# State updates as 32-row tiles and a stacked fp32r attention product in a gated-linear-attention layer

## Chip, cores and metric

One Trainium2 chip, one core. The metric is the device time of one execution in microseconds, the median of several runs. Below, PE is the engine of the matrix products (PEld its weight loader), DVE the vector engine, ACT the scalar engine, POOL the GpSimd engine, SP the engine whose queue issues most weight transfers.

## The reference

One decoder layer runs for a prompt (256 tokens) and for eight sample sequences of eight tokens each, with shared weights. The part that the change touches is the samples' gated linear attention, per head of 256 key and 512 value channels:

```python
b = jnp.cumsum(loga, axis=3)
b_last = b[:, :, :, -1:, :]
qe = q * jnp.exp(b)
ke = k * jnp.exp(-b)
kd = k * jnp.exp(b_last - b)
decay = jnp.exp(b_last[:, :, :, 0, :])
att = jnp.where(mask, jnp.einsum('nbhcd,nbhsd->nbhcs', qe, ke), 0.0)
o_intra = jnp.einsum('nbhcs,nbhse->nbhce', att, v)
def step(s, inp):
    qe_n, kd_n, v_n, dec_n = inp
    o = jnp.einsum('bhcd,bhde->bhce', qe_n, s)
    s = dec_n[..., None] * s + jnp.einsum('bhcd,bhce->bhde', kd_n, v_n)
    return s, o
```

Around it stand the input projection, the pooling branch, the merge by gates, the output projection and a SwiGLU feed-forward part; all of it is computed in float32.

## The kernel before

**The large products.** Tokens lie in the free dimension (256 of the prompt and 64 of the samples, 320 columns), channels in the partitions. Each weight chunk is split by ACT (L152) into a rounded part `whi` and by DVE (L153) into the rest `wlo`; `mm3` (L190 to L192) then makes three fp32r products of 128x128 weights with 320 columns. PE does hardly anything else from start to end. The weights come over SP's queue, in chunks into a ring of buffers.

**The heads.** While the projections of head h run (h = 1 to 3, then the output projection), the attention of the head before is worked off in steps from a queue (`gla_steps`, `pool_steps`). `pump` writes the steps between the projections, but a scheduler of the framework decides in which order each engine gets the instructions; it moves single products in between those of `mm3`. Conditioning vectors are made alongside by `ada_step` (L242, products of 128x32 column tiles on `w_ada`).

**The samples.** The eight sequences are two groups (gg) of four; each sequence has a slot of 32 partitions. `s_vstack` fills a slot with four copies of its eight value rows, in the order rounded part, rest, rounded part, rest; after the transposes of `s_nat2` that is `vp`. `s_prod` makes `kdP`, the keys that feed the state: 16 rows of rounded parts, 16 rows of rests. So one product over a slot's 32 rows gives the four cross terms.

- `s_nat3` transposes `kdP` and copies it (L886) into `kpz`: for each of the four slots j a whole 128-row array, zero outside the slot's 32 rows. Two copies on DVE and two on ACT, of 32 partitions each; the zeros are written once, on POOL (L719).
- `s_state` makes, for each group, each half d of the key channels and each sequence, one fp32r product of 128 rows and 512 columns (L957), into a PSUM tile of its own from a ring of four (`misc`), and updates the state on DVE (L959): 64 products in all, two per step.
- `s_attP` makes the scores of four sequences at once (L916) and copies them under a mask (L919) into `attP`; its rows beyond the first 16 of a slot are zero.
- `s_inter` multiplies `attP` by `vp` in float32 (L932), which PE runs as two passes, and adds the products of `qeP` with the loaded states as column tiles of 128x32, four next to each other (L936). `s_oback` copies the result out (L943) and transposes it back (L129, tile `osn`).

Other products that use less than the full array: `s_gk` (L745 and L746, 48 rows: the gate's rank and its bias) and `s_att` (L843, column tiles).

```python
PE.matmul(pt, lhsT=kpz[:, gg, j, d * P:(d + 1) * P], rhs=E["vp"][:, gg], start=True, stop=True)
...
PE.matmul(pt, lhsT=attP[:, gg], rhs=E["vp"][:, gg].bitcast(F32), start=True, stop=False,
```

Of the kernel before, what the change touches and what calls it, by code (L numbers as in the profile page):

```python
# [11 lines left out]
F32 = mybir.dt.float32  # L12
F32R = mybir.dt.float32r
I32 = mybir.dt.int32
AF = mybir.ActivationFunctionType
ALU = mybir.AluOpType
# [4 lines left out]
P = 128  # L21
TP, NB, LS = 256, 8, 8
# [6 lines left out]
H, DK, DV = 4, 256, 512  # L29
# [13 lines left out]
def shape_constants():  # L43
    s = np.arange(P)[:, None]
    c = np.arange(P)[None, :]
    m = 32 * (c // 32) + 15
    dq = ((s > m) & (s <= c)).astype(np.float32) - ((s > c) & (s <= m)).astype(np.float32)
    e = np.zeros((P, 4, 4), np.float32)
    for j in range(4):
        for i in range(j + 1, 4):  # L50
            sv = np.arange(P)
            e[:, j, i] = (sv > 32 * j + 15) & (sv <= 32 * i + 15)
    e = e.reshape(P, 16)
    after = (s > c).astype(np.float32)
    upto = (s <= c).astype(np.float32)
    m0 = np.concatenate([dq, after, e], 1)
    m1 = np.concatenate([dq, after, upto, e], 1)
    ss = np.arange(TS)[:, None]
    cs = np.arange(TS)[None, :]
    same = (ss // LS) == (cs // LS)  # L60
    ms = np.zeros((P, 2 * TS), np.float32)
    ms[:TS, :TS] = same & (ss <= cs)
    ms[:TS, TS:] = same & (ss > cs)
    inv = np.zeros((P, 4, 16), np.float32)
    for g, w in enumerate(WINDOWS):
        inv[:, g] = (1.0 / np.minimum(np.arange(16) + 1, w).astype(np.float32))[None]
    cf = np.concatenate([inv.reshape(P, 64), m0, m1, ms], 1).astype(np.float32)
    mask = (s <= c).astype(np.int32)
    r = np.arange(P)[:, None]
    q = np.arange(P)[None, :]  # L70
    mp = ((r // 32 == q // 32) & ((r % 32) < 16) & ((q % 32) < 8)
          & ((r % 8) <= (q % 32))).astype(np.int32)
    ci = np.concatenate([mask, mp], 1).astype(np.int32)
    return np.ascontiguousarray(cf), np.ascontiguousarray(ci)


NM0, NM1, NMS = 272, 400, 128
CFW = NM0 + NM1 + NMS + 64


def body(tc, A):
    nc = tc.nc
    ctx = ExitStack()
    cp = ctx.enter_context(tc.tile_pool(name="cp", bufs=1))
# [12 lines left out]
    def nm(s):  # L97
        uid[0] += 1
        return "%s_%d" % (s, uid[0])

    def misc():
        return pmisc.tile([P, 512], F32, tag="m", name=nm("pm"))
# [1 line left out]
    V, S, G, PE = nc.vector, nc.scalar, nc.gpsimd, nc.tensor  # L104


    cst = cp.tile([P, 2 * P + 64], F32, name="cst")
    msk = cp.tile([P, 2 * P], I32, name="msk")
    ident = cst[:, 0:P]
    ones = cst[:, P:2 * P]  # L110
    V.memset(ones, 1.0)
    invc = cst[:, 2 * P:2 * P + 64]
    cumr = cp.tile([P, NM0 + NM1 + NMS], F32R, name="cumr")
    M0, M1, MS = cumr[:, 0:NM0], cumr[:, NM0:NM0 + NM1], cumr[:TS, NM0 + NM1:NM0 + NM1 + NMS]
    epst = cp.tile([P, 1], F32, name="epst")
# [6 lines left out]
    vec = cp.tile([P, 4 * KT + 4], F32, name="vec")  # L122
    N1G, N2G, FG, PSC, GNG = vec[:, 0:16], vec[:, 16:32], vec[:, 32:48], vec[:, 48:64], vec[:, 64:68]
    alr = cp.tile([48, T], F32, name="alr")
    cp.tile([P, 40], F32, name="lpad")

    def tr(out, in_):
        k = in_.shape[0]
# [274 lines left out]
    with tc.tile_pool(name="head", bufs=1) as xp:  # L403
# [34 lines left out]
        pt = misc()  # L438
# [8 lines left out]
        def pinned(ins):  # L447
            tc.keep_in_program_order(ins)
# [77 lines left out]
        pt = misc()  # L526
# [118 lines left out]
        def late_loads():  # L645
            pinned(nc.gpsimd.dma_start(walr, win[:, :, OAL:OAL + 16]))
            pinned(nc.gpsimd.dma_start(msk, A["ci"]))
            pinned(nc.gpsimd.dma_start(cum, A["cf"][:, 64:CFW]))
            pinned(nc.gpsimd.dma_start(invc, A["cf"][:, 0:64]))


        plan = {}
# [60 lines left out]
    lp = mix.enter_context(tc.tile_pool(name="lp", bufs=1))  # L713
    qeP = lp.tile([P, 2, NB, 32], F32, name="qeP")
    keP = lp.tile([P, 2, NB, 32], F32, name="keP")
    kpz = lp.tile([P, 2, 4, DK], F32R, name="kpz")
    attT = lp.tile([P, 3, P], F32, name="attT")
    attP = lp.tile([P, 2, P], F32, name="attP")
    G.memset(kpz.bitcast(F32), 0.0)  # L719
    G.memset(qeP, 0.0)  # L720
    G.memset(keP, 0.0)
    G.memset(attT, 0.0)
    G.memset(attP, 0.0)

    def w4(shape, dt=F32):
        return lp.tile(shape, dt, tag="w4", bufs=4, name=nm("w4"))
# [1 line left out]
    def gla_steps(g):  # L728
        h = g.h
        st = []  # L730
        E = {}
# [57 lines left out]
        def s_prod():  # L789
            EQ, EK, EX, q, k = E["EQ"], E["EK"], E["EX"], g.q, g.k  # L790
            for d in range(2):
                V.tensor_tensor(qeP[:, d, :, 0:LS], s3(EQ[:, d, TP:T]), s3(q[:, d, TP:T]), op=ALU.mult)
                kk = s3(k[:, d, TP:T])
                V.tensor_tensor(keP[:, d, :, 0:LS], s3(EK[:, d, TP:T]), kk, op=ALU.mult)
                V.tensor_copy(E["dec"][:, d], s3(EQ[:, d, TP:T])[:, :, LS - 1])
            for d in range(2):
                G.tensor_copy(keP[:, d, :, LS:2 * LS], keP[:, d, :, 0:LS])
            V.tensor_tensor(EX[:, :, 416:480], EX[:, :, 416:480], k[:, :, TP:T], op=ALU.mult)
            kdP = E["kdP"] = w4([P, 2, NB, 32], F32R)
            for d in range(2):  # L800
                kd4 = kdP[:, d].rearrange("p b (c t) -> p b c t", t=LS)
                kd = s3(EX[:, d, 416:480]).unsqueeze(2).broadcast_to([P, NB, 2, LS])
                V.tensor_copy(kd4[:, :, 0:2, :], kd)
                V.tensor_tensor(kd4[:, :, 2:4, :], kd, kd4[:, :, 0:2, :].bitcast(F32), op=ALU.subtract)
            V.tensor_tensor(EQ[:, :, 0:TP], EQ[:, :, 0:TP], q[:, :, 0:TP], op=ALU.mult)
            V.tensor_tensor(EK[:, :, 0:TP], EK[:, :, 0:TP], k[:, :, 0:TP], op=ALU.mult)
            kq = w4([P, 2, 2, P])
            E["kdA"], E["q2"] = kq[:, 0], kq[:, 1]
            V.tensor_tensor(EX[:, :, 0:P], EX[:, :, 0:P], k[:, :, 0:P], op=ALU.mult)
            V.tensor_tensor(EX[:, :, 144:272], EX[:, :, 144:272], k[:, :, P:TP], op=ALU.mult)  # L810
            V.tensor_tensor(E["q2"], EX[:, :, 272:400], q[:, :, P:TP], op=ALU.mult)
            for d in range(2):
                V.tensor_scalar(E["kdA"][:, d], EX[:, d, 0:P], EX[:, d, 399:400], None, op0=ALU.mult)
# [58 lines left out]
        def s_nat3():  # L872
            pt = misc()
            for d in range(2):
                tr(pt[:, d * P:(d + 1) * P], E["kdA"][:, d])
                tr(pt[:, DK + d * P:DK + (d + 1) * P], E["EX"][:, d, 144:272])
            kdn = w4([P, 2, DK])
            V.tensor_copy(kdn, pt.rearrange("p (s d) -> p s d", s=2))
            pt = misc()
            for gg in range(2):  # L880
                for d in range(2):
                    tr(pt[:, gg * DK + d * P:gg * DK + (d + 1) * P],
                       E["kdP"][:, d, 4 * gg:4 * gg + 4, :].rearrange("p b r -> p (b r)").bitcast(F32))
            for j in range(4):
                r = slice(32 * j, 32 * j + 32)
                (S.copy if j % 2 else V.tensor_copy)(kpz[r, :, j, :], pt[r].rearrange("p (s d) -> p s d", s=2))  # L886
            E["kdn"] = kdn

        def s_o(e2):
# [22 lines left out]
        def s_attP():  # L912
            for gg in range(2):
                pt = misc()
                for d in range(2):
                    PE.matmul(pt[:, 0:P], lhsT=keP[:, d, 4 * gg:4 * gg + 4, :].rearrange("p b r -> p (b r)"),  # L916
                              rhs=qeP[:, d, 4 * gg:4 * gg + 4, :].rearrange("p b r -> p (b r)"),
                              start=d == 0, stop=d == 1)
                V.copy_predicated(attP[:, gg], msk[:, P:2 * P], pt[:, 0:P])  # L919

        def s_load(gg, d):
            def f():
# [6 lines left out]
        def s_inter(gg):  # L929
            def f():  # L930
                pt = E["oi"] = misc()
                PE.matmul(pt, lhsT=attP[:, gg], rhs=E["vp"][:, gg].bitcast(F32), start=True, stop=False,  # L932
                          skip_group_check=True)
                for d in range(2):
                    for j in range(4):
                        PE.matmul(pt[32 * j:32 * j + 32, :], lhsT=qeP[:, d, 4 * gg + j, :], rhs=E["S0", gg, d][:, j],  # L936
                                  start=False, stop=d == 1, tile_position=(0, 32 * j), skip_group_check=True)
            return f
# [13 lines left out]
        def s_state(gg, d, j0):  # L952
            def f():
                t = E["S0", gg, d]
                for j in (j0, j0 + 1):
                    pt = misc()
                    PE.matmul(pt, lhsT=kpz[:, gg, j, d * P:(d + 1) * P], rhs=E["vp"][:, gg], start=True, stop=True)  # L957
                    c = 4 * gg + j
                    V.scalar_tensor_tensor(t[:, j], t[:, j], E["dec"][:, d, c:c + 1], pt, op0=ALU.mult, op1=ALU.add)  # L959
                if j0 == 2:  # L960
                    nc.gpsimd.dma_start(A["o_gs"][0, 4 * gg:4 * gg + 4, h, d * P:(d + 1) * P, :]
                                        .rearrange("b p e -> p b e"), t)
            return f
# [393 lines left out]
```

## Time and profile before

| what | value |
|---|---|
| median of 3 runs | 1979.95 us (1979.15 to 1981.06) |
| the profiled execution's own time | 1981.86 us |
| its span (first to last instruction) | 1980.1 us |
| PE busy | 1946.9 us, 15080 instructions |
| PEld busy | 1857.3 us |
| DVE busy | 1014.6 us |
| ACT busy | 819.0 us |
| POOL busy | 136.5 us |

A busy time counts from an instruction's start to its modelled end. PE's products overlap, so their durations are longer than the distance between their starts; where PE's time goes is read from the starts in the timeline, and from the idle time ahead of an instruction with what ended it.

### The profile page before, as it was taken

To read this page: it belongs to the slowest core of one execution; us is meant where nothing else is said; L and a number is where in the kernel's file an instruction comes from. 1 tells how busy PE (TensorE), PEld (TensorE's weight loads), DVE (VectorE), ACT (ScalarE), POOL (GpSimd) and SP (SyncE) were. 2 spreads that over 40 slices of the span, in tenths; PEclk is the share of its full clock that TensorE was granted. 3 is DMA by queue.
4 is the path that set the end of the run, shared out by engine and by line. 5 is a ranking of instruction groups with operands and counts; after the bars stand their busy time and mean duration, and the time that the engine had idled before them with its cause. 6 is when DMAs were issued, how large, how long until landed. Compare 5 with 4: busy or idle time off the path is not lost.

```text
span 1980.1 us, 37312 instructions
## 1 busy us (share of the span) xinstructions
PE 1946.9 (98%) x15080; PEld 1857.3 (94%) x15080; DVE 1014.6 (51%) x1896; ACT 819.0 (41%) x1468; POOL 136.5 (7%) x257
## 2 busy tenths in 40 slices
PE   8999999999999999999999999999999999999997
PEld 6889998898999899889999999999999999999997
DVE  3566675575446534664574444444444444444554
ACT  3333374364345433643354333333333434344443
POOL 1112220111010101010030000000000000000000
PEclk9999999999999999999999999999999999999998
DMA  9987555776975787579656665444444444444443
GB/s 312 364 292 262 170 172 154 264 250 203 318 239 180 285 273 222 173 252 322 224 169 213 202 214 192 149 149 144 158 144 152 150 150 150 151 151 144 150 141 94
DMA packets 324607, 400.84 MB, mean 202 GB/s; under 512 B 13545, under 2 KB 264681, under 8 KB 324097
## 3 DMA queue, kind: packets, MB, share of 16 engines
q1 hardware_dynamic: 312002, 357.68, 56.2%
q0 software_dynamic: 12432, 40.77, 5.6%
q8 instruction: 118, 1.93, 0.4%
q14 instruction: 55, 0.45, 0.1%
HBM read 373.96 MB, written 24.67 MB: 201 GB/s over the span
## 4 chain that ended last, share of the span: by engine, by line
PE 94%; DMA 3%; DVE 1%; ACT 1%; issue 0%; POOL 0%; SPq 0%; POOLq 0%; DVEq 0%; ACTq 0%
PE ps L190 27%; PE ps L191 27%; PE ps L192 27%; PE pm L242 5%; DMA raw<-w_ada 1%; PE pm L129 1%; DMA raw<-w_o 1%; PE pm L936 1%; PE pm L957 1%; PE pm L905 1%; DMA raw<-w_in 1%; PE pm L435 1%; PE idle L431 1%; PE pm L932 0%; PE pm L894 0%
## 5 line engine op out<-in xcount | busy, mean ns | idle before, releaser
L153 DVE TENSOR_TENSOR wlo<-raw,whi 128x512 fp32r<-128x512 f32 x948 | 656.1, 696 | 790.7 <-ACT whi L152 787.4
L152 ACT CAST whi<-raw 128x512 fp32r<-128x512 f32 x948 | 584.4, 621 | 980.7 <-PE ps L191 865.9
L190 PE MATMUL ps<-hh,whi 128*128 128x320 f32 x1408 | 442.4, 314 | 6.6 <-ACT whi L152 5.2
L192 PE MATMUL ps<-hh,wlo 128*128 128x320 f32 x1408 | 439.2, 312 | 0.0
L191 PE MATMUL ps<-hl,whi 128*128 128x320 f32 x1408 | 438.6, 312 | 0.0
L190 PE MATMUL ps<-h2h,whi 128*128 128x320 f32 x1408 | 435.8, 310 | 0.0
L191 PE MATMUL ps<-h2l,whi 128*128 128x320 f32 x1408 | 434.9, 309 | 0.8 <-DVE h2l L1227 0.8
L192 PE MATMUL ps<-h2h,wlo 128*128 128x320 f32 x1408 | 434.8, 309 | 0.0
L190 PEld LDWEIGHTS ps<-hh,whi 128*128 128x128 f32 x1408 | 265.3, 188 | 21.6 <-issue 10.4
L191 PEld LDWEIGHTS ps<-hl,whi 128*128 128x128 f32 x1408 | 265.4, 189 | 7.2 <-issue 5.9
L192 PEld LDWEIGHTS ps<-hh,wlo 128*128 128x128 f32 x1408 | 265.2, 188 | 6.8 <-issue 5.5
L190 PEld LDWEIGHTS ps<-h2h,whi 128*128 128x128 f32 x1408 | 264.1, 188 | 2.4 <-issue 2.2
L191 PEld LDWEIGHTS ps<-h2l,whi 128*128 128x128 f32 x1408 | 264.3, 188 | 1.1 <-DVE h2l L1227 1.1
L192 PEld LDWEIGHTS ps<-h2h,wlo 128*128 128x128 f32 x1408 | 264.3, 188 | 0.0
L190 PE MATMUL ps<-ah,whi 128*128 128x320 f32 x704 | 218.5, 310 | 0.0
L192 PE MATMUL ps<-ah,wlo 128*128 128x320 f32 x704 | 217.7, 309 | 0.0
L191 PE MATMUL ps<-al,whi 128*128 128x320 f32 x704 | 217.6, 309 | 0.0
L191 PEld LDWEIGHTS ps<-al,whi 128*128 128x128 f32 x704 | 132.2, 188 | 0.0
L190 PEld LDWEIGHTS ps<-ah,whi 128*128 128x128 f32 x704 | 132.2, 188 | 0.0
L192 PEld LDWEIGHTS ps<-ah,wlo 128*128 128x128 f32 x704 | 132.2, 188 | 0.0
L242 PE MATMUL pm<-raw,scT 128*32 128x128 f32 (+1 forms) x2688 | 101.5, 293 | 4.3 <-DMA raw<-w_ada 4.3
L242 PEld LDWEIGHTS pm<-raw,scT 128*32 128x32 f32 x2688 | 72.0, 110 | 25.7 <-issue 13.4
(315 smaller groups left out, 1569.3 us busy)
## 6 DMA issues: line engine op xcount, KB each, us to landing
raw<-w_ada SPq DMA_DIRECT2D x192, 512.0 KB, 6.3
raw<-w_gu SPq DMA_DIRECT2D x176, 512.0 KB, 3.5
raw<-w_in SPq DMA_DIRECT2D x173, 512.0 KB, 4.3
raw<-w_down SPq DMA_DIRECT2D x79, 512.0 KB, 3.4
S<-state_gla POOLq DMA_DIRECT2D x16, 1024.0 KB, 8.9
o_gs<-S POOLq DMA_DIRECT2D x16, 1024.0 KB, 7.3
raw<-w_o SPq DMA_DIRECT2D x32, 512.0 KB, 5.6
raw<-w_down SPq DMA_DIRECT2D x15, 256.0 KB, 2.5
```

What stands on the lines that cost most here:

```text
L129: PE.transpose(out, in_, ident[:k, :k])
L152: S.copy(hi, raw)
L153: V.tensor_sub(lo, raw, hi.bitcast(F32))
L190: PE.matmul(ps, lhsT=whi, rhs=xhi, start=start, stop=False)
L191: PE.matmul(ps, lhsT=whi, rhs=xlo, start=False, stop=False)
L192: PE.matmul(ps, lhsT=wlo, rhs=xhi, start=False, stop=stop)
L242: ins = PE.matmul(ps[32 * j:32 * j + 32, 0:w], lhsT=scT[:, k, :], rhs=raws[j], start=k == 0 if start is None else start, stop=k == KT - 1 ...
L431: tc.keep_in_program_order(PE.matmul(idle[:, 0, :], lhsT=fill[:, 0:P], rhs=fill, start=True, stop=True))
L435: tc.keep_in_program_order(PE.transpose(out, in_, ident[:k, :k]))
L905: PE.matmul(pt, lhsT=E["kdn"][:, s, d * P:(d + 1) * P], rhs=E["vn"][:, s], start=s == 0, stop=s == 1)
L936: PE.matmul(pt[32 * j:32 * j + 32, :], lhsT=qeP[:, d, 4 * gg + j, :], rhs=E["S0", gg, d][:, j], start=False, stop=d == 1, tile_position=(0 ...
L957: PE.matmul(pt, lhsT=kpz[:, gg, j, d * P:(d + 1) * P], rhs=E["vp"][:, gg], start=True, stop=True)
```

## The change

1. `kpz` and its zeros go. One ACT copy (L887 after) puts the transposed keys into `kp`, 128 partitions with the four slots below each other.
2. `s_state` takes two PSUM tiles and issues its two products on the slots' 32 partitions alone, as row tiles (`tile_position=(32 * j, 0)`), and then the two updates.
3. The keys of the scores (`keP`) are repeated over all four parts of a slot instead of two, by POOL, and the mask keeps all 32 rows. `ahl` holds the masked scores. ACT rounds them into `attP` (L921), ACT makes `ah`, the rounded part with a sign by row (L923), and DVE combines (L924), so that the first 16 rows of a slot hold the rounded scores and the last 16 the rest. With `vp` as it was, one fp32r product then gives the four cross terms (L937).

```diff
-    kpz = lp.tile([P, 2, 4, DK], F32R, name="kpz")
+    kp = lp.tile([P, 2, DK], F32R, name="kp")
+    ahl = lp.tile([P, 2, P], F32, name="ahl")
...
-                G.tensor_copy(keP[:, d, :, LS:2 * LS], keP[:, d, :, 0:LS])
+                G.tensor_copy(keP[:, d].rearrange("p b (c t) -> p b c t", t=LS)[:, :, 1:4, :],
+                              keP[:, d, :, 0:LS].unsqueeze(2).broadcast_to([P, NB, 3, LS]))
...
-            for j in range(4):
-                r = slice(32 * j, 32 * j + 32)
-                (S.copy if j % 2 else V.tensor_copy)(kpz[r, :, j, :], pt[r].rearrange("p (s d) -> p s d", s=2))
+            S.copy(kp, pt.rearrange("p (s d) -> p s d", s=2))
...
-                V.copy_predicated(attP[:, gg], msk[:, P:2 * P], pt[:, 0:P])
+                V.copy_predicated(ahl[:, gg], msk[:, P:2 * P], pt[:, 0:P])
+                S.copy(attP[:, gg], ahl[:, gg])
+                t = lp.tile([P, P], F32, tag="acc", name=nm("ah"))
+                S.activation(t, attP[:, gg].bitcast(F32), AF.Copy, scale=adds)
+                V.scalar_tensor_tensor(attP[:, gg], ahl[:, gg], takes, t, op0=ALU.mult, op1=ALU.add)
...
-                PE.matmul(pt, lhsT=attP[:, gg], rhs=E["vp"][:, gg].bitcast(F32), start=True, stop=False,
+                PE.matmul(pt, lhsT=attP[:, gg], rhs=E["vp"][:, gg], start=True, stop=False,
...
-                for j in (j0, j0 + 1):
-                    pt = misc()
-                    PE.matmul(pt, lhsT=kpz[:, gg, j, d * P:(d + 1) * P], rhs=E["vp"][:, gg], start=True, stop=True)
+                pts = [misc() for _ in range(2)]
+                for j, pt in zip((j0, j0 + 1), pts):
+                    r = slice(32 * j, 32 * j + 32)
+                    PE.matmul(pt, lhsT=kp[r, gg, d * P:(d + 1) * P], rhs=E["vp"][r, gg], start=True, stop=True,
+                              tile_position=(32 * j, 0))
+                for j, pt in zip((j0, j0 + 1), pts):
                     c = 4 * gg + j
                     V.scalar_tensor_tensor(t[:, j], t[:, j], E["dec"][:, d, c:c + 1], pt, op0=ALU.mult, op1=ALU.add)
```

The rest of the diff makes the mask and the two columns of row signs (`takes`, `adds`), loads them, and drops the zero fill.

**The order of the instructions.** PE in the first head, second half of the key channels, before (L957 is a state product, L190 to L192 are projections, `ps` is their result):

```order
L190 MATMUL ps_3934<-hh_93,whi_3953 128x320
L191 MATMUL ps_3934<-hl_803,whi_3953 128x320
L957 MATMUL pm_3862<-vp_3578,kpz 128x512
L192 MATMUL ps_3934<-hh_93,wlo_3954 128x320
L190 MATMUL ps_3934<-hh_94,whi_3971 128x320
L191 MATMUL ps_3934<-hl_1184,whi_3971 128x320
L957 MATMUL pm_3865<-vp_3578,kpz 128x512
L192 MATMUL ps_3934<-hh_94,wlo_3972 128x320
```

and after (L963 is the state product, L192 to L194 the projections):

```order
L192 MATMUL ps_3939<-hh_93,whi_3958 128x320
L193 MATMUL ps_3939<-hl_803,whi_3958 128x320
L963 MATMUL pm_3865<-vp_3578,kp 128x512
L194 MATMUL ps_3939<-hh_93,wlo_3959 128x320
L192 MATMUL ps_3939<-hh_94,whi_3976 128x320
L193 MATMUL ps_3939<-hl_1184,whi_3976 128x320
L963 MATMUL pm_3870<-vp_3578,kp 128x512
L194 MATMUL ps_3939<-hh_94,wlo_3977 128x320
```

Nothing moved here: the products still stand one by one between projections, now as row tiles.

PE in the second head, behind the transposes of `s_oback`, before:

```order
L190 MATMUL ps_5218<-hh_96,whi_5271 128x320
L129 MATMUL pm_4713<-cst,osn_4711 128x128 x4
L957 MATMUL pm_4722<-vp_4664,kpz 128x512
L957 MATMUL pm_4725<-vp_4664,kpz 128x512
L957 MATMUL pm_4728<-vp_4664,kpz 128x512
L191 MATMUL ps_5218<-hl_1245,whi_5271 128x320
```

and after (L131 are the transposes):

```order
L192 MATMUL ps_5228<-hh_97,whi_5281 128x320
L131 MATMUL pm_4723<-cst,osn_4721 128x128 x4
L963 MATMUL pm_4732<-vp_4669,kp 128x512
L963 MATMUL pm_4733<-vp_4669,kp 128x512
L963 MATMUL pm_4738<-vp_4669,kp 128x512
L193 MATMUL ps_5228<-hl_1269,whi_5281 128x320
```

The run of three state products stays a run of three, two projections later.

ACT in the first head, where the scores' new steps come in, after (L154 are the weight casts):

```order
L154 CAST whi_3792<-raw_3790 128x512
L887 CAST kp<-pm_3598 128x512
L921 CAST attP<-ahl 128x128 x2
L923 ACTIVATE ah_3609<-attP,cst 128x128
L154 CAST whi_3808<-raw_3790 128x512
L923 ACTIVATE ah_3617<-attP,cst 128x128
L154 CAST whi_3942<-raw_3940 128x512
```

Before, two copies to `kpz` stood among these casts, and nothing for the scores.

## Rows read from the trace of the kernel before

**Rows 1.** The page: busy time by engine, and the chain that ended last.
```profile
PE 1946.9 (98%) x15080; PEld 1857.3 (94%) x15080; DVE 1014.6 (51%) x1896; ACT 819.0 (41%) x1468; POOL 136.5 (7%) x257
...
PE 94%; DMA 3%; DVE 1%; ACT 1%; issue 0%; POOL 0%; SPq 0%; POOLq 0%; DVEq 0%; ACTq 0%
```

**Rows 2.** PE's groups by form: busy us, mean ns | idle before.
```profile
L957 PE MATMUL pm<-vp,kpz 128*128 128x512 f32 x64 | 23.2, 405 | 0.0
...
L932 PE MATMUL pm<-vp,attP 128*128 128x512 f32 x16 | 8.3, 598 | 0.0
```

**Rows 3.** Timeline of PE around a state product: start us, us, instruction.
```profile
347.18 0.31 PE L191 MATMUL ps<-hl,whi 128*128 128x320 f32 x1
347.32 0.39 PE L957 MATMUL pm<-vp,kpz 128*128 128x512 f32 x1
347.56 0.31 PE L192 MATMUL ps<-hh,wlo 128*128 128x320 f32 x1
347.70 0.31 PE L190 MATMUL ps<-hh,whi 128*128 128x320 f32 x1
```

**Rows 4.** The tile kpz: ns min/median/max, and idle before (us, times).
```profile
L957 PEld LDWEIGHTS pm<-vp,kpz x64: 186/188/192, 338.7 to 870.8; 128*128 128x128 f32 x64
...
L886 DVE CAST kpz<-pm x8: 671/684/690, 327.3 to 820.5; 32x512 fp32r<-32x512 f32 x8
L886 ACT CAST kpz<-pm x8: 576/577/579, 328.0 to 821.2; 32x512 fp32r<-32x512 f32 x8
...
  issue: 0.2, 1
```

**Rows 5.** Timeline of PE around the gate stage of a head.
```profile
587.32 0.31 PE L190 MATMUL ps<-hh,whi 128*128 128x320 f32 x1
587.56 1.13 PE L745 MATMUL pm<-wa,alr 48*128 48x256 f32 x4
588.62 0.64 PE L746 MATMUL pm<-wa,alr 48*64 48x256 f32 x2
589.19 0.41 PE L191 MATMUL ps<-hl,whi 128*128 128x320 f32 x1
589.44 0.31 PE L192 MATMUL ps<-hh,wlo 128*128 128x320 f32 x1
```

**Rows 6.** Timeline of DVE, PE and PEld around the first head's attention product.
```profile
328.79 0.48 DVE L919 COPY_PREDICATED attP<-msk,pm 128x128 f32<-128x128 int32 x2
...
331.77 0.31 PE L191 MATMUL ps<-hl,whi 128*128 128x320 f32 x1
...
331.92 1.02 PE L932 MATMUL pm<-vp,attP 128*128 128x512 f32 x2
...
332.87 1.92 PE L936 MATMUL pm<-S,qeP 128*32 128x512 f32 x16
...
334.72 0.19 PEld L192 LDWEIGHTS ps<-hh,wlo 128*128 128x128 f32 x1 [0.84 <-issue]
334.72 0.41 PE L192 MATMUL ps<-hh,wlo 128*128 128x320 f32 x1
...
334.97 0.31 PE L190 MATMUL ps<-hh,whi 128*128 128x320 f32 x1
```

**Rows 7.** Waits of the weight loader: us in total, times, longest.
```profile
PEld pm L242 <- issue: 13.4, 66, 0.4
PEld pm L936 <- issue: 7.9, 21, 0.8
...
PEld pm L746 <- issue: 1.3, 4, 0.3
```

**Rows 8.** ACT's groups by form, 235 to 900 us.
```profile
L851 ACT COPY attT<-pm 128x128 f32<-128x128 f32 x4 | 1.1, 265 | 8.9 <-PE pm L848 8.9
```

**Rows 9.** Waits of PE: us in total, times, longest.
```profile
PE pm L242 <- DMA raw<-w_ada: 4.3, 3, 2.3
...
PE ps L190 <- ACT mh L327: 0.9, 1, 0.9
```

More of the change, by code (lines that the diff above doesn't have):

```diff
@@ L66, in shape_constants @@
         inv[:, g] = (1.0 / np.minimum(np.arange(16) + 1, w).astype(np.float32))[None]
-    cf = np.concatenate([inv.reshape(P, 64), m0, m1, ms], 1).astype(np.float32)
+    lo = s % 32 >= 16
+    parts = np.concatenate([lo, 1 - 2.0 * lo], 1)
+    cf = np.concatenate([inv.reshape(P, 64), parts, m0, m1, ms], 1).astype(np.float32)
     mask = (s <= c).astype(np.int32)
@@ L70, in shape_constants @@
     q = np.arange(P)[None, :]
-    mp = ((r // 32 == q // 32) & ((r % 32) < 16) & ((q % 32) < 8)
-          & ((r % 8) <= (q % 32))).astype(np.int32)
+    mp = ((r // 32 == q // 32) & ((q % 32) < 8) & ((r % 8) <= (q % 32))).astype(np.int32)
     ci = np.concatenate([mask, mp], 1).astype(np.int32)
@@ L77 @@
 NM0, NM1, NMS = 272, 400, 128
-CFW = NM0 + NM1 + NMS + 64
+CFW = NM0 + NM1 + NMS + 66
 def body(tc, A):
@@ L104, in body @@
     V, S, G, PE = nc.vector, nc.scalar, nc.gpsimd, nc.tensor
-    cst = cp.tile([P, 2 * P + 64], F32, name="cst")
+    cst = cp.tile([P, 2 * P + 72], F32, name="cst")
     msk = cp.tile([P, 2 * P], I32, name="msk")
@@ L111, in body @@
     V.memset(ones, 1.0)
-    invc = cst[:, 2 * P:2 * P + 64]
+    invc = cst[:, 2 * P:2 * P + 66]
+    takes, adds = cst[:, 2 * P + 64:2 * P + 65], cst[:, 2 * P + 65:2 * P + 66]
     cumr = cp.tile([P, NM0 + NM1 + NMS], F32R, name="cumr")
@@ L124, in body @@
     alr = cp.tile([48, T], F32, name="alr")
-    cp.tile([P, 40], F32, name="lpad")
+    cp.tile([P, 32], F32, name="lpad")
     def tr(out, in_):
@@ L647, in late_loads @@
             pinned(nc.gpsimd.dma_start(msk, A["ci"]))
-            pinned(nc.gpsimd.dma_start(cum, A["cf"][:, 64:CFW]))
-            pinned(nc.gpsimd.dma_start(invc, A["cf"][:, 0:64]))
+            pinned(nc.gpsimd.dma_start(cum, A["cf"][:, 66:CFW]))
+            pinned(nc.gpsimd.dma_start(invc, A["cf"][:, 0:66]))
         plan = {}
@@ L715, in body @@
     keP = lp.tile([P, 2, NB, 32], F32, name="keP")
-    kpz = lp.tile([P, 2, 4, DK], F32R, name="kpz")
+    kp = lp.tile([P, 2, DK], F32R, name="kp")
+    ahl = lp.tile([P, 2, P], F32, name="ahl")
     attT = lp.tile([P, 3, P], F32, name="attT")
-    attP = lp.tile([P, 2, P], F32, name="attP")
-    G.memset(kpz.bitcast(F32), 0.0)
+    attP = lp.tile([P, 2, P], F32R, name="attP")
     G.memset(qeP, 0.0)
@@ L722, in body @@
     G.memset(attT, 0.0)
-    G.memset(attP, 0.0)
+    G.memset(ahl, 0.0)
     def w4(shape, dt=F32):
```

## The prediction

> **What bounds the kernel now.** I read the page first: TensorE (PE) is busy for 98% of the span and holds 94% of the chain that ended last [rows 1]. The two other engines that the change touches, DVE and ACT, have half of their time free, so a microsecond of theirs costs nothing unless PE waits for it. The question is therefore what each edit does to the stream of PE instructions, and second whether PE is made to wait.
>
> The groups by form give the instructions concerned [rows 2]: 64 state products (L957), and 8 attention products (L932) that show as 16, since each float32 product runs as two passes. Their busy times overlap with their neighbours', so I don't use the "mean ns"; what an instruction costs is how far it pushes the next start apart. The timeline shows that for a state product [rows 3]: projection products of 320 columns start 0.14 to 0.15 us apart; the one after a state product starts 0.24 us later, which in the other places is 0.23. A state product thus costs 0.23 us, and its weight load hides beside the product before it: in the view of one tile, the engine's idle time ahead of all 64 weight loads is 0.2 us [rows 4].
>
> The third view is the timeline where PE leaves the full 128x128 array for a smaller tile and comes back [rows 5]. In a head's gate stage it goes from 320-column products to products of 48 rows (L745, 48*128) and 48*64 (L746). The first start comes 0.24 us after the last projection instead of 0.15: 0.09 to enter. The four L745 passes take 1.06 us until L746 starts; at half of the 0.43 us that a 512-column float32 pass takes [rows 6] they need 0.86, so 0.20 is on top: a first weight load that nothing hides (0.10), and the change to the next tile shape (0.10). After L746 the first projection runs 0.25 us until the next start instead of 0.15: its load is bare again, 0.10. The same shows around the column tiles of L936: 0.84 us of idle weight loader ahead of the projection that follows, and 0.25 us for that projection [rows 6]. So one visit to a smaller tile costs about 0.09 to enter, 0.10 for the first load, 0.09 to leave and 0.10 for the first full load: **0.38 us a visit**, whatever is computed in it. The waits say it in sum: "issue" (nothing that the profile shows) ahead of weight loads of L242, L936 and L746, all of them entries into a smaller tile, is 13.4, 7.9 and 1.3 us [rows 7].
>
> **The change, part by part.** *State products.* A zero-filled 128-row product becomes a 32-row tile. It still streams 512 columns, so alone it saves nothing: the zeros cost no time before. What can be saved is overlap, where two such tiles stand next to each other on different rows; what is paid is the visit. The code issues them in pairs, but the order shown above is what PE gets: the scheduler puts projections between the two of a pair. Counted through the four heads, the 64 products stand in 47 runs: 38 alone, one run of two, eight runs of three. Before there were 47 runs too, so the overlap has 17 followers (1 + 8 x 2) and the visit is paid 47 times.
>
> Followers: taken as free, since the four column tiles of L936 do run together (16 passes in 1.85 us until the next projection starts, against 16 x 0.43 = 6.9 one after the other) [rows 6]. Row tiles side by side stand in no row of this trace, so the ends are 0.23 us saved each and nothing: 17 x 0.23 = 3.9 us saved, or 0. I take 3.9. The Trainium skill (TensorE: Matmul & The Clock Gate, "Measured speedup vs the span model") puts a packed neighbour at about 4 ns on top of one product; by it the 3.9 would be 3.8.
>
> Visits: 47 x 0.38 = 17.9 us. The price is that of a 48-row tile, the nearest row; a 32-row tile may differ. The lower end is 0 (a row tile might be entered as freely as L957 is now), the upper 0.45, which allows 0.07 for a load that its own 32 rows cannot hide. I take 0.38. State products in all: 17.9 - 3.9 = +14.0 us.
>
> *Attention times v.* Before, L932 starts at 331.92 and the column tiles at 332.87: 0.95 us [rows 6], two passes of 0.43 and the entry of 0.09. After, one fp32r pass of 512 columns, 0.21 to 0.23 as in rows 3, and the same entry: 0.31. Saved 0.64 us, 8 times: **-5.1 us**. Ends: 0.60 to 0.66 each, -4.8 to -5.3.
>
> *The longer chain to it.* Now mask copy, then a cast on ACT, a scaled copy on ACT and a combining step on DVE, before L932's successor may start. Before, the mask copies end at 329.27 and PE takes the product at 331.92: 2.65 us of slack in the first head [rows 6]. The new steps are two of 0.27 us on ACT (L851, same size) [rows 8] and one on DVE, at 0.24 by the mask copies [rows 6]; in the order one weight cast and one wlo stand between them at worst, about as long as a kpz copy (0.68) [rows 4]: some 2.2 us. The product itself stands 5 projections later than before (0.7 us). PE finds it done: 0, with ends 0 and +0.5 in each head, +2.0 together.
>
> *Free work.* The four kpz copies per head (0.68 on DVE, 0.58 on ACT [rows 4]) give way to one ACT copy; over the program ACT and DVE change by some 2 to 3 us each way, on engines that are half idle. The memset and the wider copy on POOL are off PE's path by tens of us. 0.
>
> *Waits that may shrink.* If PE is slower, transfers it waited for come less late: PE waited 4.3 us for w_ada in three places, the longest 2.3, and 0.9 for mh at the end of the last head [rows 9]. The 2.3 lies behind the heads. At most 2.0 + 0.9 would go; the loads are issued when PE frees the buffer, so they move with it. I take 0, ends -2.9 and 0.
>
> **Sum.** 14.0 - 5.1 = +8.9 us. Against the profiled execution's own 1981.86 us that is 1990.8; the median of the three runs shown is 1.9 below it, and from 1979.95 it is **1988.9 us**. About 0.2% (4.0 us) is what a measurement of this kernel can tell from no change; this is twice that. With x for the price of a visit the sum is 47x - 3.9 - 5.1, which is zero at x = 0.19 us: half of what the rows show decides the sign.
>
> **Rivals.** *(1) Row tiles are entered without the visit's price.* Lone 32-row products then cost their 0.23 as before, and the change gives 3.9 + 5.1 = 9.0 us: 1971.0, faster. It decides where x falls clearly below 0.19. For it speaks that no row read here is of a 32-row tile with 128 columns. Against it: 48*128 pays, 48*64 pays and the column tiles pay. The Trainium skill (TensorE: Matmul & The Clock Gate, "Why this matters for your kernels") recommends this very slicing for small contractions, with four tiles at 3.07 times one after the other; the page names no price for a lone tile between full products.
>
> *(2) Half of the price.* If the two weight loads hid and only entering and leaving stayed, a visit would cost 0.18: 47 x 0.18 - 9.0 = -0.5 us, 1979.4, no change. L746's smaller load, some 0.05 us of its 0.57 [rows 5], speaks a little for it; the bare 0.25 after each visit speaks against it.
>
> *(3) Followers don't overlap.* The three of a run stand on different rows but each waits for its own result bank, which DVE must have freed. Then the 3.9 is lost: 17.9 - 5.1 = +12.8 us, 1992.8. Before, PE had no idle time ahead of any of the 64 [rows 2], so the banks come free in time, and I hold it for unlikely.
>
> **How the numbers follow.** Forecast (x from 0.30 to 0.45, followers free) 0.65; rival (3) 0.13; rival (2) 0.11; rival (1) 0.11. The forecast's own range is 47 x 0.30 - 9.0 = +5.1 to 47 x 0.45 - 9.0 + 2.0 = +14.2, that is 1985.0 to 1994.1; rival (3) lies inside it. Waits that shrink take up to 2.9 off the lower end, and part of rival (3) at the dearer visit lies above: the range is 1982.0 to 1995.0, and leaves out (1) and (2), 0.22. Slower by over 0.2% (beyond 1983.9): forecast and (3), 0.78; within: (2), 0.11; faster: (1), 0.11.
>
> **What would show it.** In the timeline after, a lone state product: 0.24 us from the projection before it, 0.40 to the next, then 0.25, together 0.89 where it is 0.52 now. "Issue" ahead of the state products' weight loads goes from 0.2 us to some 5 or more, and the same grows ahead of the projections behind them. A run of three takes no longer than one alone. L932 shows 8 times instead of 16, and 0.31 us before the column tiles. No wait of PE for attP. The forecast is wrong if the product after a lone state product still starts 0.23 us later, or if PE waits for DVE or ACT ahead of the attention product.

## The result and the profile after

| | before | after |
|---|---|---|
| median of 9 runs, us | 1980.30 (1977.21 to 1981.17) | 1984.87 (1983.20 to 1987.36) |
| ratio, 95% interval | | 1.0024 [1.0015, 1.0033] |
| profiled execution, own time, us | 1981.86 | 1985.18 |
| its span, us | 1980.1 | 1983.4 |

The change makes the kernel 4.6 us slower by the medians, where 8.9 were forecast. Sums below go by medians: of the 30 runs of before beside the first four experiments, five lie at 1987 to 1989 us and pull the ratios given with those down by up to a thousandth.

The page of after answers to [rows 1]: busy time, and the chain.

```profile
PE 1953.4 (98%) x15072; PEld 1850.2 (93%) x15072; DVE 1013.7 (51%) x1896; ACT 822.3 (41%) x1480; POOL 135.8 (7%) x256
...
PE 95%; DMA 2%; ACT 1%; DVE 1%; issue 0%; POOL 0%; SPq 0%; POOLq 0%; DVEq 0%; ACTq 0%
```

TensorE is busy 6.5 us longer, and the span is only 3.3 longer; so part of what the change costs was taken from TensorE's idle time. Both halves of that sentence are followed here. First the groups by form, answering to [rows 2] (busy us, mean ns | idle before):

```profile
L963 PE MATMUL pm<-vp,kp 32*128 32x512 f32 x64 | 23.3, 494 | 0.0
L937 PE MATMUL pm<-vp,attP 128*128 128x512 f32 x8 | 3.5, 442 | 0.0
```

The attention product shows 8 times now, not 16. The state products' busy time is what it was (23.3 against 23.2), since busy time overlaps with the neighbours'; as before, only the start times tell the price. The timeline of after around a state product that stands alone (start us, us, instruction):

```profile
347.02 0.31 PE L192 MATMUL ps<-hh,whi 128*128 128x320 f32 x1
347.17 0.31 PE L193 MATMUL ps<-hl,whi 128*128 128x320 f32 x1
347.41 0.49 PE L963 MATMUL pm<-vp,kp 32*128 32x512 f32 x1
347.83 0.41 PE L194 MATMUL ps<-hh,wlo 128*128 128x320 f32 x1
348.08 0.31 PE L192 MATMUL ps<-hh,whi 128*128 128x320 f32 x1
```

From the projection to the state product 0.24 us, from there to the next projection 0.42, from that to the one after 0.25. Before, the same three steps took 0.14, 0.24 and 0.14 [rows 3]. The visit costs 0.91 - 0.52 = 0.39 us. The same holds for all 38 lone products: 0.233 to 0.240 us, 0.419 to 0.430, and 0.249 to 0.257 (twice 0.37, where a float32 product of 320 columns, L981, follows). And around a run of three:

```profile
378.77 0.60 PE L131 MATMUL pm<-cst,osn 128*128 128x128 f32 x4
379.30 0.50 PE L963 MATMUL pm<-vp,kp 32*128 32x512 f32 x3
379.74 0.42 PE L194 MATMUL ps<-hh,wlo 128*128 128x320 f32 x1
379.99 0.31 PE L192 MATMUL ps<-hh,whi 128*128 128x320 f32 x1
```

Three row tiles take 0.44 us until the next projection starts, one takes 0.42. Within a run they start 3 to 4 ns apart, all 17 times. The attention product, answering to [rows 6]:

```profile
332.19 0.31 PE L192 MATMUL ps<-hh,whi 128*128 128x320 f32 x1
332.33 0.39 PE L937 MATMUL pm<-vp,attP 128*128 128x512 f32 x1
332.65 0.64 PE L941 MATMUL pm<-S,qeP 128*32 128x512 f32 x4
```

It is 0.32 us to the column tiles, 0.95 before. The waits of the weight loader answer to [rows 7] (us in total, times, longest):

```profile
PEld ps L192 <- issue: 18.9, 63, 0.8
PEld pm L244 <- issue: 12.9, 65, 0.4
PEld ps L193 <- issue: 11.5, 33, 0.8
PEld pm L963 <- issue: 6.7, 36, 0.2
...
PEld pm L941 <- issue: 6.0, 21, 0.6
PEld ps L194 <- issue: 5.6, 24, 0.2
```

L963 is the entry into the row tile (0.2 us for L957 before); L192 to L194 are the projections, whose loads are bare when the visit ends. These three add up to 36.0 us in 120 places; before, the same three projections had 25.2 us in 78:

```profile
PEld ps L190 <- issue: 13.4, 48, 0.8
...
PEld ps L191 <- issue: 6.3, 16, 0.8
PEld ps L192 <- issue: 5.5, 14, 0.8
```

Second, what came back. The waits of PE in after, the row that answers to [rows 9]:

```profile
PE pm L244 <- DMA raw<-w_ada: 0.9, 2, 0.4
```

The wait for w_ada was 4.3 us before; the 0.9 us for mh is gone from the list. To see where, I cut both traces at the same instructions: the start of one w_ada product ahead of the heads (216.93 us in before), the first product of the output projection, and the last one. The columns are the stretch, its us, the busy us (and instructions) of PE, PEld, DVE, ACT and POOL, PE's granted clock, the DMA share and GB/s. Before:

```profile
216.93:876.29 659.36, 653.37 (x5325) 599.27 (x5324) 376.74 (x750) 306.67 (x578) 83.53 (x142) 1.00 0.69 226
876.29:1012.34 136.05, 132.66 (x1189) 128.02 (x1186) 73.28 (x158) 48.21 (x93) 5.88 (x16) 0.99 0.80 264
```

After:

```profile
216.51:884.30 667.79, 662.78 (x5316) 594.55 (x5315) 377.68 (x751) 309.80 (x590) 82.83 (x141) 1.00 0.68 224
884.30:1015.45 131.15, 131.04 (x1190) 126.86 (x1186) 71.09 (x158) 48.32 (x93) 5.89 (x16) 1.00 0.81 271
```

In the heads TensorE works 9.4 us longer (662.78 - 653.37), and is idle 1.0 us less (5.01 against 5.99). The output projection, which the change does not touch, is 4.9 us *shorter*: 3.39 us of idle time are now 0.11, and 1.6 us of busy time are gone. That last part is the clock. Ten-microsecond stretches of before, same columns:

```profile
317.00:327.00 10.00, 9.36 (x58) 9.31 (x59) 7.53 (x23) 4.14 (x7) 0.00 (x0) 0.83 0.30 90
907.00:917.00 10.00, 7.63 (x79) 6.69 (x78) 5.10 (x13) 4.10 (x8) 1.36 (x2) 0.83 1.04 362
```

At 907 us PE waits 2.3 us for w_ada, and in the same stretch the granted clock, at 1.00 (the level of 2.4 GHz) before, leaves that level for a while (0.83 in the mean; 0.50, the level of 1.2 GHz, from 912 to 914 us): 10 x 0.17 = 1.7 us lost. After has 1.00 there. The dip at 317 us, ahead of the state products, is in both.

### The profile page after: what moved, and what is told of

Its sections match the earlier page's. It is cut to its first block, busy times and chain, and to the rows that moved or that the text cites. A ratio compares the mean times of both kernels' runs of the same rounds, so it can differ in the third digit from the quotient of the medians.

```text
span 1983.4 us, 37295 instructions
## 1 busy us (share of the span) xinstructions
PE 1953.4 (98%) x15072; PEld 1850.2 (93%) x15072; DVE 1013.7 (51%) x1896; ACT 822.3 (41%) x1480; POOL 135.8 (7%) x256
## 4 chain that ended last, share of the span: by engine, by line
PE 95%; DMA 2%; ACT 1%; DVE 1%; issue 0%; POOL 0%; SPq 0%; POOLq 0%; DVEq 0%; ACTq 0%
PE ps L192 28%; PE ps L193 27%; PE ps L194 27%; PE pm L244 5%; PE pm L131 1%; DMA raw<-w_ada 1%; PE pm L963 1%; PE pm L941 1%; PE pm L906 1%; DMA raw<-w_in 1%; DMA xn<-x_prompt 1%; PE pm L437 0%; PE pm L895 0%; PE pm L778 0%; PE pm L779 0%
## 5 line engine op out<-in xcount | busy, mean ns | idle before, releaser
L154 ACT CAST whi<-raw 128x512 fp32r<-128x512 f32 x948 | 584.7, 621 | 984.4 <-PE ps L193 878.5
L192 PE MATMUL ps<-hh,whi 128*128 128x320 f32 x1408 | 443.4, 315 | 7.0 <-ACT whi L154 5.5
L194 PE MATMUL ps<-hh,wlo 128*128 128x320 f32 x1408 | 440.3, 313 | 0.0
L192 PE MATMUL ps<-h2h,whi 128*128 128x320 f32 x1408 | 435.8, 310 | 0.0
L194 PE MATMUL ps<-h2h,wlo 128*128 128x320 f32 x1408 | 434.8, 309 | 0.0
L192 PEld LDWEIGHTS ps<-hh,whi 128*128 128x128 f32 x1408 | 265.3, 188 | 27.0 <-issue 15.7
L194 PEld LDWEIGHTS ps<-hh,wlo 128*128 128x128 f32 x1408 | 265.2, 188 | 6.1 <-issue 5.4
L192 PEld LDWEIGHTS ps<-h2h,whi 128*128 128x128 f32 x1408 | 264.0, 188 | 2.4 <-issue 2.2
L194 PEld LDWEIGHTS ps<-h2h,wlo 128*128 128x128 f32 x1408 | 264.2, 188 | 0.0
L192 PE MATMUL ps<-ah,whi 128*128 128x320 f32 x704 | 218.5, 310 | 0.0
L194 PE MATMUL ps<-ah,wlo 128*128 128x320 f32 x704 | 217.7, 309 | 0.0
L193 PEld LDWEIGHTS ps<-al,whi 128*128 128x128 f32 x704 | 132.2, 188 | 0.0
L192 PEld LDWEIGHTS ps<-ah,whi 128*128 128x128 f32 x704 | 132.2, 188 | 0.0
L194 PEld LDWEIGHTS ps<-ah,wlo 128*128 128x128 f32 x704 | 132.1, 188 | 0.0
```

The source lines that it names most:

```text
L154: S.copy(hi, raw)
L192: PE.matmul(ps, lhsT=whi, rhs=xhi, start=start, stop=False)
L193: PE.matmul(ps, lhsT=whi, rhs=xlo, start=False, stop=False)
L194: PE.matmul(ps, lhsT=wlo, rhs=xhi, start=False, stop=stop)
```

## The experiments

Two theories stood after this. **A**: the heads cost what was forecast, and the delay takes away a wait and a slow-clock stretch that any delay would take away. **B**: what came back belongs to the other order of the instructions. A third, **C**, came with the first results: the output projection's length varies from execution to execution, whatever the kernel.

**One half of the change at a time.** *attn_only* puts before's full-array state products back into the change:

```diff
-    kp = lp.tile([P, 2, DK], F32R, name="kp")
+    kpz = lp.tile([P, 2, 4, DK], F32R, name="kpz")
...
-                    PE.matmul(pt, lhsT=kp[r, gg, d * P:(d + 1) * P], rhs=E["vp"][r, gg], start=True, stop=True,
-                              tile_position=(32 * j, 0))
+                    PE.matmul(pt, lhsT=kpz[:, gg, j, d * P:(d + 1) * P], rhs=E["vp"][:, gg], start=True, stop=True)
```

(with its four copies and its memset; `ahl` becomes one tile for both groups and `lpad` goes, so that it fits).

> The stacked fp32r attention product alone; the state products stay full-array with zero-filled keys. Sum of the prediction: TensorE 0.64 us x 8 = 5.1 us less than before. Theory A (the heads cost what was forecast, and what came back behind them is the 2.3 us wait for w_ada at 908 us of the trace of before and the slow-clock stretch behind it): a TensorE that is 5 us earlier meets that wait again and waits longer, so of the 5.1 us little is kept: -0 to -3 us against before, with a wait for w_ada of 2 to 6 us and a granted clock below 1 after it. Theory B (what came back is the other order of the instructions, not the delay): the gain is kept, -5 us.

Measured: 1973.84 us beside 1979.76 of before, **-5.9**; ratio 0.9959 [0.9943, 0.9975]. *rows_only* is before with the change's `kp` and `s_state`, and the old attention product:

> The 32-row state tiles alone, with the two-pass attention product of before. Sum of the prediction: 47 visits x 0.38 us less 17 followers x 0.23 us = +14.0 us. Theory A: the delay takes away the w_ada wait at 908 us and the slow-clock stretch behind it, some 4.9 us, so +9 us against before, no w_ada wait over 1 us and a granted clock of 1.00 in the stretch where before had 0.68. Theory B (the order returns the time, and this has other runs of the scheduler): anything between +9 and +14; +14 if nothing is returned.

Measured: 1990.35, **+10.6**; ratio 1.0045 [1.0030, 1.0060]. The two halves add up to +4.7, and the change measured +4.6. Their stretches, rows_only first:

```profile
214.05:887.82 673.77, 669.18 (x5325) 597.46 (x5324) 376.42 (x744) 306.08 (x574) 81.52 (x141) 0.99 0.66 222
887.82:1020.19 132.37, 131.28 (x1189) 126.85 (x1186) 70.94 (x157) 48.58 (x93) 7.70 (x16) 1.00 0.79 265
```

attn_only:

```profile
215.36:867.10 651.74, 647.15 (x5316) 596.28 (x5315) 379.45 (x758) 311.59 (x594) 86.22 (x142) 1.00 0.68 228
867.10:1001.25 134.15, 131.43 (x1190) 126.92 (x1186) 73.46 (x158) 48.44 (x93) 5.88 (x16) 1.00 0.80 268
```

The busy time in the heads has to be freed of slow-clock stretches before it is compared. rows_only has two in the heads, 1.7 us each; one of them stands at 267 to 287 us, where before has none and no state product has run yet:

```profile
267.00:277.00 10.00, 8.63 (x53) 7.96 (x52) 7.27 (x11) 9.91 (x17) 2.70 (x4) 0.96 0.36 102
277.00:287.00 10.00, 10.00 (x60) 9.73 (x59) 6.71 (x9) 7.38 (x13) 1.57 (x1) 0.87 0.46 142
```

and attn_only has none at all, not even the one at 317 that before and the change show:

```profile
317.00:327.00 10.00, 10.00 (x76) 9.98 (x75) 8.83 (x23) 5.10 (x10) 0.00 (x0) 1.00 0.35 108
```

At the full clock rows_only works 669.18 - 3.4 = 665.8 us in the heads, before 653.37 - 1.7 = 651.7: **+14.1, forecast +14.0**. attn_only works 647.2: **-4.5, forecast -5.1**. So the prices of the two parts were right, but the second saves 0.6 us less. For the slower half the total fits A (+9) only roughly, since of its 14.1 us 3.5 came back, and it lies in B's range (+9 to +14) too. For the faster half A fails and B (-5) is met: the 4.5 us were kept whole, and PE's wait for w_ada in the output projection was 1.2 us, not 2 to 6, with no clock below 1.00 behind it. So A in the form "a fixed schedule of transfers takes up any shift of TensorE" falls.

**Delay without the change.** *dummy* puts a 256-column product ahead of each state product of before:

```diff
+                    PE.matmul(pt[:, 0:256], lhsT=kpz[:, gg, j, d * P:(d + 1) * P], rhs=E["vp"][:, gg, 0:256], start=True, stop=True)
                     PE.matmul(pt, lhsT=kpz[:, gg, j, d * P:(d + 1) * P], rhs=E["vp"][:, gg], start=True, stop=True)
```

> Before, with one more full-array product of 256 columns ahead of each of the 64 state products (its result is overwritten): no smaller tile, no other attention, only TensorE later. 64 x about 0.107 us (256 columns at 2.4 GHz) = +6.8 us of TensorE in the heads. Theory A: the first 4.9 us of any delay come back at the start of the output projection, so about +2 us against before, and the w_ada wait and the slow-clock stretch are gone from the trace. Theory B (the return belongs to the order of the change): +6.8 us, and the wait stands where it stood.

Measured: 1990.68, **+10.9**; ratio 1.0046 [1.0032, 1.0060]: both theories missed. The added products push the next start 0.113 to 0.120 us apart in 55 of the 64 places and 0.20 to 0.23 us in the other nine, 8.2 us in all and not the 6.8 expected, and the heads' busy time rises by 8.0 (661.33 against 653.37, each with one slow-clock stretch). The w_ada wait behind the heads did shrink, as A has it, to 0.5 us. The waits of PE from 886 to 966 us:

```profile
PE ps L190 <- DVE mg L1064: 2.4, 1, 2.4
PE ps L190 <- ACT whi L152: 0.6, 1, 0.6
PE pm L242 <- DMA raw<-w_ada: 0.5, 1, 0.5
```

But TensorE now stands 2.4 us for `mg`, the merge on DVE of the last head, and the clock is at 0.83 in the 10 us behind that. One wait at this seam went and another came. So a delay of this size need not return anything; why `mg` is late here was not followed.

**The price by runs or by tiles.** *pairs* is the change with every two products side by side:

```diff
+                    if last:
+                        tc.add_manual_dep(ps[0].ins, last[-1].ins.name, mybir.DependencyInfo(
+                            mybir.DependencyClass.Sync, mybir.DependencyReason.ANTI), reason="slots")
+                    for p in ps[1:]:
+                        tc.keep_in_program_order(p)
+                    last.append(us[-1])
```

> The change, with its 64 state products always issued as 32 runs of two adjacent row tiles (the first of a pair waits for the last state update of the pair before, the second stands behind it) in place of 38 singles, one pair and 8 triples. If a run costs 0.38 us for the visit and each follower saves 0.23 us: 32 x 0.38 - 32 x 0.23 = +4.8 us where the change has +14.0, and with the attention product's -5.1 a TensorE sum of -0.3 against before. Theory A: as TensorE is as early as in before, the w_ada wait is back, so -1 to +1 us against before and about 4 us faster than the change. Rival on the visit (the cost is per tile and not per run, so that grouping gains nothing): no faster than the change, +4 to +5 us against before. Theory B (the order returns the time): with the change's kind of order some 5 us returned as well, -5 us.

Measured: 1980.98, **+1.2**; ratio 0.9998 [0.9984, 1.0012]. The order became 32 runs of two, and the timeline (columns as above) shows one visit for both:

```profile
382.46 0.31 PE L193 MATMUL ps<-hl,whi 128*128 128x320 f32 x1
382.70 0.49 PE L965 MATMUL pm<-vp,kp 32*128 32x512 f32 x2
383.12 0.41 PE L194 MATMUL ps<-hh,wlo 128*128 128x320 f32 x1
383.38 0.30 PE L192 MATMUL ps<-hh,whi 128*128 128x320 f32 x1
```

In the groups by form the 64 products now overlap with each other, 16.0 us busy where the change has 23.3:

```profile
L965 PE MATMUL pm<-vp,kp 32*128 32x512 f32 x64 | 16.0, 496 | 0.0
```

and on the page PE is busy for 1944.0 us against 1953.4 in the change: 9.4 less, where the sums differ by 8.9 + 0.3 = 9.2:

```profile
PE 1944.0 (98%) x15072; PEld 1848.2 (93%) x15072; DVE 1014.4 (51%) x1896; ACT 824.0 (42%) x1480; POOL 136.8 (7%) x256
```

The price is per run: the rival (per tile) falls, and so does B's -5. A's total is nearly met (-1 to +1), but not by its mechanism: the w_ada wait in the output projection is 0.2 us here and did not come back. Of the 9.4 us only 3.4 to 3.9 reached the median. The trace has 33.0 us of idle PE in its span (1977.0 - 1944.0) where the change has 30.0, so 6.4 us stand between the two spans; and the profiled execution of pairs lies 2.2 us below the median of its runs, which reach from 1976.87 to 1987.22 us. Forcing the order also moved 48 w_ada products from the heads into the output projection, so its stretches can't be set against the others'.

**The w_ada wait taken away by itself.** *before_late* and *after_late* issue the 16 reloads of the residual input (`x1`) two at a time ahead of each column tile, so that w_ada stands earlier in SP's queue; *attn_late* does so in attn_only:

```diff
-    for k in range(KT):
-        nc.sync.dma_start(x1[k], xspill[k])
...
     for ui in range(7):
         ps = proj(wo, 256 * ui, 0, KT, mh, ml)
+        reload(2 * ui, 2 * ui + 1)
```

> Before, with the 16 reloads of the residual input spread over the output projection (two ahead of each column tile) in place of all 16 ahead of it, so that the w_ada loads are issued earlier. TensorE's work is the same. Theory A: the 2.3 us w_ada wait at 908 us and the slow-clock stretch behind it go without any delay in the heads: -3 to -4.5 us against before, granted clock 1.00 in the stretch. Theory B (the wait is not what came back): within 1 us of before.

Measured: 1978.39 us beside 1979.71, **-1.3**; ratio 0.9988 [0.9978, 0.9998]. The direction is A's, the size less than half; the interval reaches from -0.4 to -4.4 us, so that it excludes neither A's -3 nor B's "within 1 us".

> The change with the same spread reloads. Theory A: the change has no such wait left, so it stays within 1 us of the change, and its distance to before with spread reloads is the full price of the heads, +8 to +10 us (forecast +8.9), where it was +4.6. Theory B: both kernels move alike and the distance stays near +4.6.

Measured: 1985.61, **+5.9** over before and 0.7 above the change's 1984.87, within A's 1 us; ratio 1.0023 [1.0013, 1.0033]. The distance to before_late is 7.2 us: more than 4.6, as A has it, and short of its 8 to 10. The profiled execution took 1992.91 us, 7.3 above the median, so no row of its trace is read here.

> The stacked attention product alone, full-array state products, and the spread reloads. Theory A: the 5.1 us of the attention product are kept now, -5 us against before with spread reloads and -8 to -10 against before: the fastest of all. Theory B: -5 against before.

Measured: 1971.39 us (5 runs), **-8.3**; ratio 0.9950 [0.9933, 0.9968]: the fastest kernel here, 13 us faster than the change. A had -8 to -10, B -5. In the heads it works 650.30 us with two slow-clock stretches of 1.7, so 646.9 at the full clock: attn_only's 647.2 again.

**Is the stretch the kernel's, or chance?** The first trace of before_late lay 2.5 us under the median of its runs, so one trace of each kernel was not enough. Four more, of kernels that had run already:

> The kernel before, unchanged, profiled once more. From the first product of the output projection to its last one the first trace of before took 136.1 us, that of the change 131.1. Theory A (the stretch is the kernel's own: a late w_ada and the slow clock behind it): about 136 us again, w_ada wait over 2 us, granted clock below 0.8 in the 5 us behind it. Rival C (the stretch varies by some us from execution to execution, whatever the kernel): anything from 131 to 137.

> The kernel before, unchanged, profiled a third time. Theory A: 136 us in that stretch, and heads of 659 us. Rival C: 131 to 137 us in that stretch; heads of 659 us under both.

> The change, unchanged, profiled a second time. Heads 668 us, 8 to 9 us over before, under both. Theory A: 131 us in the output projection, without a wait for w_ada there. Rival C: 131 to 137 us.

> Before with the spread reloads, profiled a second time (the first trace was 2.5 us below the median of its runs, with 131.7 us in the output projection). Theory A: about 132 us again. Rival C: 131 to 137 us.

Cut at the same instructions (us; the clock's loss is 10 us x 0.17 for each stretch of 10 us at 0.83):

| trace | heads: PE busy | lost to the clock | busy at full clock | PE idle | output projection | PE idle there |
|---|---|---|---|---|---|---|
| before | 653.4 | 1.7 | 651.7 | 6.0 | 136.1 | 3.4 |
| before_2 | 653.4 | 1.7 | 651.7 | 5.8 | 134.8 | 3.5 |
| before_3 | 655.1 | 3.4 | 651.7 | 7.8 | 133.3 | 2.0 |
| after | 662.8 | 1.7 | 661.1 | 5.0 | 131.1 | 0.1 |
| after_2 | 662.7 | 1.7 | 661.0 | 4.6 | 132.2 | 0.1 |
| rows_only | 669.2 | 3.4 | 665.8 | 4.6 | 132.4 | 1.1 |
| attn_only | 647.2 | 0 | 647.2 | 4.6 | 134.2 | 2.7 |
| attn_late | 650.3 | 3.4 | 646.9 | 4.8 | 132.6 | 0.9 |

The work at full clock repeats to 0.1 us in the kernels traced more than once: +9.4 us for the change, each time. The idle time does not repeat. The waits of before_3 between 860 and 920 us show why:

```profile
PE ps L190 <- DVE mg L1063: 1.3, 1, 1.3
PE ps L190 <- ACT mh L327: 1.0, 1, 1.0
PE ps L190 <- ACT whi L152: 0.6, 1, 0.6
PE ps L192 <- DVE wlo L153: 0.2, 1, 0.2
```

w_ada is not among them, where before has 2.3 and before_2 1.9 us for it; `mg`, `mh` and the weight casts are. The 1.3 us for `mg` lie just ahead of the first product of the output projection, so the table has them in the heads. before_2 has the wait and no slow clock behind it. after_2 is 1.1 us longer than after in the output projection with the same idle time; there it is the clock, 0.89 in the last 10 us. before_late_2 has the waits for mh (1.4), w_ada (0.4) and mg (0.3), and 132.9 us in the output projection; so the spread reloads take the w_ada wait nearly away in both traces, and leave those for mg and mh. Both A and C are partly right: the seam between heads and output projection costs before 2.0 to 3.5 us of idle time in the output projection in all three traces, and the change 0.1 in both; which wait it is, and whether the clock falls behind it, changes from execution to execution. The two halves, each with an order of its own, add up to +4.7 against +4.6, so there is no sign of a return that only the change's own order makes, though each half is known to some 3 us only.

But one part of what came back is not the delay's. Here is PE's wait for w_ada inside the heads (us, times, longest), in before, in dummy (TensorE 8.0 us later by the end of the heads) and in attn_only (4.5 us less work than before):

```profile
PE pm L242 <- DMA raw<-w_ada: 2.1, 2, 1.1
PE pm L242 <- DMA raw<-w_ada: 1.7, 3, 1.1
PE pm L243 <- DMA raw<-w_ada: 0.5, 1, 0.5
```

It is 1.9 and 2.2 in before_2 and before_3, 0.9 and 0.4 in after and after_2, 0.5 in rows_only and 0.6 in attn_late. So it shrinks by some 1.4 us in the change and in either half of it, whether TensorE is later or earlier, and hardly by a delay alone. That is B's kind of return; what in these programs does it was not tried.

## Why the prediction was right, and where its size was off

- *The visit* (0.38 us, 47 times): right. 0.39 in the timeline, the three parts 0.24, 0.42 and 0.25 where 0.24, 0.40 and 0.25 were named; and by runs, not by tiles (pairs).
- *Followers free* (17): right, 3 to 4 ns each. The Trainium skill ("TensorE: Matmul & The Clock Gate", Measured speedup vs the span model) has about 4 ns; the trace agrees. Rival (3) falls.
- *State products +14.0*: +14.1 in rows_only. Rivals (1) and (2) fall with it: nothing of the visit is free here.
- *Attention -5.1*: -4.5 and -4.8 in two traces, where -4.8 to -5.3 was named, so up to 0.6 us too much. Six of the eight products stand 0.32 us ahead of the next instruction; one stands at 0.73, having started 0.03 us behind a float32 product (L906), and one 0.23 us ahead of a projection. Where the 0.3 to 0.6 us are lost was not followed.
- *The longer chain to the attention product at 0*: right; no wait of PE for attP is in the list.
- *The sum +8.9*: the heads' work rose by 9.4.
- *"Waits that may shrink ... I take 0, ends -2.9 and 0"*: **this step failed**, and it is why the total is half of the forecast. It allowed for 2.0 + 0.9 us at most, set the 2.3 us wait for w_ada aside since it "lies behind the heads", and held that loads "move with" PE. Of the 2.0 inside the heads more than half went, the 0.9 went, and so did the 2.3. In the table, idle time of 2.0 to 3.5 us in the output projection became 0.1, and that in the heads fell from 6.0, 5.8 and 7.8 to 5.0 and 4.6. In the means that is -2.9 and -1.7, and 9.4 - 2.9 - 1.7 = +4.8; measured +4.6. So close a match is partly luck, with three traces against two: the mean spans of the same traces differ by 3.7. A slow-clock stretch of 1.7 us behind the wait, in one of three traces of before, is the rest of why the first pair of profiles shows only +3.3.
- *Why the waits shrank* is shown in part only. That a delay takes the waits behind the heads fits the change (no wait left) and rows_only (0.2 us for w_ada); but before_3 has none for w_ada without any delay, attn_only has 1.2 with TensorE earlier, and dummy got another wait in its place. The fall inside the heads comes without a delay too (attn_only).
- *The range, 1982.0 to 1995.0*: 1984.87 lies in it only by the 2.9 us that it takes off for such waits. The forecast's own range began at 1985.0. The direction and the price of the heads were understood; the total was met less well than its two parts.

The transfers did not move with PE. The two w_ada loads were issued 903.18 us into before and 908.78 into after, 5.6 us later, while the first product of the output projection is 8.0 us later; and they took less time to land. The issues of before:

```profile
raw<-w_ada SPq DMA_DIRECT2D x2, 512.0 KB, 6.8
```

and of after, 5.6 us later (median us from issue to landing at the end):

```profile
raw<-w_ada SPq DMA_DIRECT2D x2, 512.0 KB, 4.7
```

Why SP's reloads, which stand ahead of these, began only 5.6 us later was not tried, nor which transfers the shorter landing escaped.

## What to carry to other kernels

A small row tile alone between full-array products has a price that is paid per run of such tiles, not per tile; count the runs in the order that the engine really gets. Here a run costs 0.39 us and each follower in it gives back 0.23, so by an estimate from these two a run must have three tiles to break even; where most stand alone, a zero-filled full-array product is the cheaper one (here 14 us of 1980). A change with a good part and a bad part is best taken apart: the attention half alone, with its loads spread, is 8.3 us faster than before. And when a change makes the bound engine later, list every wait downstream and price each as a possible return, those behind the changed stage above all; but don't count on it, since another late result may take the place of the first (dummy), and the wait may come and go between executions of one kernel (before_3).

## What the runs showed of the hardware

The slow-clock stretches in the heads and the output projection come in one size: each costs 1.7 us (0.83 in the mean of 10 us). Most stand behind pauses of TensorE of 1.4 to 2.4 us, but not behind each such pause: at 317 us in seven of the eight traces of the table (attn_only is the exception), behind the pause at 270 us in three (before_3, rows_only, attn_late), behind the w_ada wait in before and not in before_2, whose 10 us there hold 2.6 us of idle time against 2.4. And two stand behind no such pause: the 10 us from 1011 us in after_2 and from 999 us in attn_late have 0.83 as well, with 0.1 us of idle TensorE in them and none in the 20 us ahead. A comparison of two traces at a few microseconds has to take such stretches out first; here that turned -6.2 and -3.1 us for the same attention product into -4.5 and -4.8.
